# A trunk layer in split fp32: who splits the weights of the up product, the third branch and the projection, and who sums the stored blocks

## The chip, the cores and the metric

One core of a Trainium2 chip. The time is the device time of one execution in microseconds (us). The core's engines run side by side and meet through semaphores: TensorE (PE, matmuls into PSUM), VectorE (DVE), ScalarE (ACT), GpSimd (POOL), and SyncE (SP), whose queue issues most of the DMA transfers.

## The reference, cut to what matters

One decoder layer on x of 1024 tokens by 1024 features: three attention mixers, whose outputs pass a branch product each and are gated and summed, an output projection, and a squared-ReLU MLP. The change touches the end of the layer:

```python
y = jnp.einsum('nbsm,nmd->bsnd', branches, w_branch[layer])
gate = jax.nn.sigmoid(mg.reshape(B, S, N_BRANCH, D_MODEL).astype(jnp.float32)).astype(y.dtype)
x = x + jnp.sum(gate * y, axis=2) @ w_out[layer]

h = rms_norm(x, norm_mlp[layer])
x = x + jnp.square(jax.nn.relu(h @ w_up[layer])) @ w_down[layer]
```

All of it is fp32; w_branch[2] is the third branch, w_out the projection, w_up the up product (1024 by 4096).

## The kernel before, in words

**Splits.** Every fp32 operand of a matmul is split into a high and a low part: ScalarE casts the high part (L90), then VectorE or GpSimd subtracts it from the source (L91). `split` takes the engine as its last argument, `weight` loads a block and splits it, GpSimd being its default. A product then takes three matmuls, L119, L120 and L121. In the traces the high part of a weight is wh, the low part wl, a loaded raw block wr, a sum of blocks s.

**Third branch and projection.** The third branch (loop over two halves of the tokens and eight blocks d of features, L1230 and after) takes a weight, a gate g and a product, multiplies them (L1233), adds to y (L1235), and splits y into mh and ml (L1236, L1237). The projection's weights wo (eight blocks of two halves each, split at L1291) are loaded and split in the same stretch, and the projection itself follows.

**The up product.** w_up is cut into H = 16 pairs p. Each pair is one 2x2-block product done by a Strassen-like scheme with seven products, numbered 1 to 7; some take a raw block of w_up, others a sum of blocks (`sums`, L1267). A product is four steps of k with three matmuls each, 12 matmuls on 128x512 tiles. Products 2, 7 and 3 go on in the PSUM bank of products 1, 6 and 5, so before TensorE starts product 7 of a pair VectorE must have read product 6 out of the bank (L1416, u2 = product 6 + e1), and before product 3 it must have read product 5 (L1423, behind L1421, which reads product 7). Product 4 is added at L1426, product 3 at L1429, ScalarE applies ReLU and square (L1435, L1436). `store` then sums the finished blocks of the pair (again L1267, u from u) and sends the seven blocks to the DRAM tiles ud on SP's queue; SP's queue also loads the blocks of w_up.

**Order.** For the first HEAD = 4 pairs the products 1, 2 and 4 are done first, from raw blocks; then TensorE runs 6, 5, 7 of pair 0, 6 of pair 1, 3 of pair 0, 5 and 7 of pair 1, 6 of pair 2, 3 of pair 1, and so on; from pair 4 the products run pair by pair. TensorE's order is written by hand. Every other engine's order is set by a scheduler that plans the program on a timeline. `tc.issue_after(ins)` is a hold: what is written inside it stands behind `ins` in the order of the engine that runs `ins` (VectorE here); it doesn't wait for the end of `ins`. Before the change the products 6, 5, 7, 3 of the four pairs are held behind `last["sum"]` (L1332), the last sum of the activations' blocks.

**Buffers.** The raw blocks wr have 7 buffers, the sums s 5, the split weights 11 (3 + 8), the temporaries u 12, the copies of product 4 v 4. Each engine takes its instructions strictly in its own order.

Of the kernel before, what the change touches and what calls it, by code (L numbers as in the profile page):

```python
# [14 lines left out]
ALU = mybir.AluOpType  # L15
# [60 lines left out]
class Kernel:  # L76
# [1113 lines left out]
    def merge_and_mlp(self):  # L1190
        tc, nc, a = self.tc, self.nc, self.a
        kw = dict(bufs=1, reuse_waits="tile")
        halves = [slice(0, 512), slice(512, 1024)]
        mp = tc.alloc_tile_pool(name="mp", side="left", **kw)
        mh = mp.tile([P, KT, S], F32R, name="mh")
        ml = mp.tile([P, KT, S], F32R, name="ml")
        pre = tc.alloc_tile_pool(name="pre", side="right", **kw)
        self.wp = pre
        self.w_n, self.wr_bufs, self.w_bufs = 512, 3, 3
        with (tc.tile_pool(name="bb", side="right", **kw) as bb, tc.tile_pool(name="br", side="right", **kw) as br,  # L1200
              tc.tile_pool(name="bl", side="left", **kw) as bl, tc.tile_pool(name="bg", side="left", **kw) as bg,
              tc.tile_pool(name="wx", side="left", **kw) as wx):
            self.other = wx
            ob = [[bb.tile([P, S], F32R, name=f"ob{i}{x}") for x in range(2)] for i in range(4)]
            oc = [None, None]
            y = [None, None]
            for half, pool in ((0, br), (1, bl)):
                y[half] = pool.tile([P, KT, 512], F32, name="y")
                oc[half] = [[pool.tile([P, 512], F32R, name=f"oc{i}{x}") for x in range(2)] for i in range(4)]
            for s in halves:  # L1210
                for i in range(4):
                    self.operand(self.od[4 + i], s, *[x[:, s] for x in ob[i]])
            for d in range(KT):
                w = self.weight(a["wbr"][1, d], 512)
                if d == 1:
                    self.wo_after = self.last_load
                for half, s in enumerate(halves):
                    g = self.gate(bg, "g", 3, 1, d, s)
                    with tc.issue_after(self.last_gate):
                        nc.sync.dma_start(y[half][:, d], self.yd[d, :, s])  # L1220
                    ps = self.branch(1, d, [x[0][:, s] for x in ob], [x[1][:, s] for x in ob], w)
                    nc.vector.scalar_tensor_tensor(g, g, 1.0, ps, op0=ALU.add, op1=ALU.mult)
                    v = y[half][:, d, :]
                    nc.gpsimd.tensor_tensor(v, v, g, op=ALU.add)
            for half, s in enumerate(halves):
                for i in range(4):
                    self.operand(self.od[8 + i], s, *oc[half][i])
            for half, s in enumerate(halves):
                for d in range(KT):
                    w = self.weight(a["wbr"][2, d], 512)  # L1230
                    g = self.gate(bg, "g", 3, 2, d, s)
                    ps = self.branch(2, d, [x[0] for x in oc[half]], [x[1] for x in oc[half]], w)
                    nc.vector.scalar_tensor_tensor(g, g, 1.0, ps, op0=ALU.add, op1=ALU.mult)  # L1233
                    v = y[half][:, d, :]
                    nc.vector.tensor_tensor(v, v, g, op=ALU.add)  # L1235
                    nc.scalar.activation(mh[:, d, s], v, AF.Copy, scale=0.5)  # L1236
                    nc.vector.scalar_tensor_tensor(ml[:, d, s], v, 0.5, mh[:, d, s].bitcast(F32),  # L1237
                                                   op0=ALU.mult, op1=ALU.subtract)

        self.tail(mp, mh, ml, halves, pre)  # L1240
# [33 lines left out]
    def tail(self, mp, mh, ml, halves, pre):  # L1274
        tc, nc, a = self.tc, self.nc, self.a
# [9 lines left out]
        wo = [[wps[k // 4].tile([P, D], F32R, name=f"wo{k}{x}") for x in range(2)] for k in range(KT)]  # L1285
        for k in range(KT):
            r = xp.tile([P, D], F32, name="x1", tag="x1", bufs=2)
            with tc.issue_after(self.wo_after):
                nc.sync.dma_start(r, a["wo"][k])
            for s in halves:  # L1290
                self.split(wo[k][0][:, s], wo[k][1][:, s], r[:, s], nc.vector if k % 2 else nc.gpsimd)  # L1291
        nc.sync.dma_start(g, a["norm_mlp"].broadcast_to([P, D]))


# [43 lines left out]
        last = {}  # L1338
        HEAD = 4
# [24 lines left out]
        def form():  # L1364
            count["f"] += 1
            pool, bufs = (pre, 3) if main is None or count["f"] % 11 < 3 else (main, 8)
            return [pool.tile([P, 512], F32R, name=f"w{x}", tag=f"w{x}", bufs=bufs) for x in "hl"]
# [11 lines left out]
        def temp(tag="u"):  # L1379
            pool, bufs = dict(u=(more, 12), v=(more, 4), s=(main, 5), e=(main, HEAD))[tag]  # L1380
            return pool.tile([P, 512], F32, name=tag, tag=tag, bufs=bufs)

        def splitted(src, eng):
            f = form()
            self.split(*f, src, eng)
            return f
# [4 lines left out]
        def up_pair(p):  # L1391
            o = Pair()
            wu = lambda n: raw(a["wu"][p + H * (n[0] == "2"), :, (int(n[1]) - 1) * 512:int(n[1]) * 512])
            get = self.sums(wu, lambda: temp("s"), "s", nc.vector)
            o.ps, o.p4 = {}, None
            o.n = 0

            def product(i, chain=None, again=False):

                name = self.ASIDE[i]  # L1400
                w = splitted(wu(name) if again else get(name), nc.gpsimd)
                bh, bl, k0, s = moving[self.BSIDE[i]]
                ps = o.ps[i] = o.ps[chain] if chain else self.mm()
                for k in range(4):
                    ks = slice(k * P, k * P + P)
                    self.mm3(ps, w[0][:, ks], w[1][:, ks], bh[:, k0 + k, s], bl[:, k0 + k, s],
                             k == 0 and not chain, k == 3, bool(chain))

            def after(i):

                if i == 1:
                    o.e1 = temp("e")
                    nc.scalar.activation(o.e1, o.ps[1], AF.Copy)
                elif i == 6:
                    o.u2 = temp()
                    nc.vector.tensor_tensor(o.u2, o.ps[6], o.e1, op=ALU.add)  # L1416
                elif i == 2:
                    o.c11 = act(o.ps[2])
                elif i == 7:
                    u3 = o.u3 = temp()  # L1420
                    nc.vector.tensor_tensor(u3, o.ps[7], o.e1, op=ALU.add)  # L1421
                    c = temp()
                    nc.vector.tensor_tensor(c, o.ps[5], u3, op=ALU.add)  # L1423
                    o.c22 = act(c)
                elif i == 4:
                    nc.vector.tensor_tensor(o.u3, o.p4 or o.ps[4], o.u3, op=ALU.add)  # L1426
                    o.c21 = act(o.u3)
                elif i == 3:
                    nc.vector.tensor_tensor(o.u2, o.ps[3], o.u2, op=ALU.add)  # L1429
                    o.c12 = act(o.u2)  # L1430
                    store()

            def act(c):
                u = temp()
                nc.scalar.activation(u, c, AF.Relu)  # L1435
                nc.scalar.activation(u, u, AF.Square)  # L1436
                return u

            def store():

                blocks = {"11": o.c11, "12": o.c21, "21": o.c12, "22": o.c22}
                get = self.sums(lambda n: blocks[n], temp, "s", nc.vector)
                for i in self.ORDER:
                    nc.sync.dma_start(ud[p][i], get(self.ASIDE[i]))

            o.product, o.after = product, after
            return o

# [6 lines left out]
        pairs = [up_pair(p) for p in range(HEAD)]  # L1455
# [17 lines left out]
        for o in pairs:  # L1473
            o.product(4, None, True)
            o.p4 = temp("v")
            nc.scalar.activation(o.p4, o.ps[4], AF.Copy)
        with tc.issue_after(last["sum"]):
            for i, o in enumerate(pairs):
                up(o, (6,))
                if i:  # L1480
                    up(pairs[i - 1], (3,))
                up(o, (5, 7))
                o.after(4)
# [28 lines left out]
        for b in range(0, H, G):  # L1512
# [7 lines left out]
            for i in LAST if final else order:  # L1520
# [5 lines left out]
                if b and rest and count["x"] % 2 == 0:  # L1526
                    t, s = rest.pop(0)
                    r = main.tile([P, 512], F32, name="xr", tag="e", bufs=HEAD)
# [6 lines left out]
                for j in range(4):  # L1535
# [19 lines left out]
                    t, s = place[i](j)  # L1555
# [70 lines left out]
```

## Time and profile before

| | us |
|---|---|
| median of 3 runs | 1986.71 |
| the three runs | 1987.52, 1983.32, 1986.71 |
| the profiled execution | 1990.27 |
| its span in the trace | 1988.5 |
| PE busy | 1879.6 |
| DVE busy | 1420.5 |
| ACT busy | 1013.7 |
| POOL busy | 976.5 |

Times in the trace count from the start of the span. The third branch runs in about 1210 to 1255, the projection to about 1360, the up product's first four pairs from there to about 1440.

### The profile page before, as it was taken

The numbers are of one execution on the slowest core, as the hardware profiler recorded it, in microseconds if no ns is written. First come the engines' busy times: TensorE is split into PE (matmuls) and PEld (weight loads), VectorE is DVE, ScalarE is ACT, GpSimd is POOL, SyncE is SP. The second block draws the span as 40 slices with busy tenths as digits, with TensorE's granted clock in tenths as the row PEclk, the third lists the DMA queues.
The fourth block names the chain that finished last, engine by engine and source line by source line (L and its number), as shares of the span: only waits on it lengthen the run. The fifth ranks groups of instructions, "written<-read, shape, count | busy, mean of one in ns | idle before, by whom it ended". The sixth has DMA issues, their size and how long they took to land. (4 is left out here: it accounts for less than half of the span.)

```text
span 1988.5 us, 30626 instructions
## 1 busy us (share of the span) xinstructions
PE 1879.6 (95%) x9842; PEld 1611.2 (81%) x9842; DVE 1420.5 (71%) x3196; ACT 1013.7 (51%) x2566; POOL 976.5 (49%) x1146
## 2 busy tenths in 40 slices
PE   7999999998899999999999889999899999999998
PEld 6888889887688888888888778887688888887886
DVE  7747777788657677658776756657755446899988
ACT  5456555666546555536556533335455546543432
POOL 4455455643361122172222237328454555889787
PEclk9999999999999999999999899999999999999999
DMA  6132012101201111202342557425544446455443
GB/s 225 52 107 57 9 57 55 53 16 55 84 27 63 52 52 58 79 19 93 100 127 94 172 168 256 158 86 166 170 170 158 147 155 207 159 179 181 129 154 111
DMA packets 124924, 221.58 MB, mean 111 GB/s; under 512 B 14708, under 2 KB 35732, under 8 KB 124764
## 3 DMA queue, kind: packets, MB, share of 16 engines
q1 hardware_dynamic: 123180, 213.87, 33.0%
q10 hardware_dynamic: 1584, 5.77, 0.9%
q8 instruction: 77, 1.26, 0.3%
q14 instruction: 83, 0.68, 0.1%
HBM read 158.68 MB, written 64.83 MB: 112 GB/s over the span
## 5 line engine op out<-in xcount | busy, mean ns | idle before, releaser
L91 POOL TENSOR_TENSOR wl<-wr,wh 128x512 fp32r<-128x512 f32 (+3 forms) x246 | 329.3, 1345 | 264.6 <-ACT wh L90 212.7
L90 ACT ACTIVATE wh<-wr 128x512 fp32r<-128x512 f32 (+3 forms) x258 | 149.9, 589 | 183.4 <-PE mm L120 111.9
L716 PE MATMUL sc<-st 128*128 128x256 f32 (+6 forms) x736 | 182.5, 341 | 20.8 <-ACT p L748 20.1
L90 ACT ACTIVATE ph<-tr 128x384 fp32r<-128x384 f32 (+3 forms) x280 | 138.6, 497 | 118.6 <-PE tr L764 97.5
L91 DVE TENSOR_TENSOR pl<-tr,ph 128x384 fp32r<-128x384 f32 (+3 forms) x280 | 155.7, 559 | 33.1 <-ACT ph L90 31.1
L119 PE MATMUL mm<-hh,wh 128*128 128x512 f32 x384 | 159.0, 414 | 0.0
L761 POOL MEMSET ph<- 128x128 f32 x152 | 33.7, 222 | 252.3 <-PE ac L904 220.1
L716 PEld LDWEIGHTS sc<-st 128*128 128x128 f32 x736 | 122.1, 191 | 41.0 <-ACT p L748 32.0
L120 PE MATMUL mm<-hl,wh 128*128 128x512 f32 x384 | 151.6, 395 | 0.0
L121 PE MATMUL mm<-hh,wl 128*128 128x512 f32 x384 | 151.5, 395 | 0.0
L119 PE MATMUL mm<-wh 128*128 128x512 f32 x352 | 138.2, 393 | 3.4 <-DVE x L1499 3.4
L120 PE MATMUL mm<-wl,wh 128*128 128x512 f32 x352 | 138.3, 393 | 2.1 <-POOL wl L91 2.0
L90 ACT ACTIVATE wh<-u 128x512 fp32r<-128x512 f32 x158 | 90.7, 621 | 93.2 <-PE tr L120 35.0
L121 PE MATMUL mm<-wh,wl 128*128 128x512 f32 x352 | 137.9, 392 | 0.0
L764 PE MATMUL tr<-ident,p 128*128 128x128 f32 x792 | 128.8, 275 | 8.7 <-DVE st L569 7.4
L91 POOL TENSOR_TENSOR wl<-s,wh 128x512 fp32r<-128x512 f32 x68 | 94.8, 1401 | 77.6 <-ACT wh L90 76.6
L748 ACT ACTIVATE p<-sc,mc 128x256 f32<-128x256 f32 (+5 forms) x200 | 106.7, 539 | 47.2 <-DVE mc L740 43.1
L904 PE MATMUL ac<-ph,st 128*128 128x256 f32 x392 | 109.8, 298 | 19.6 <-DVE ob L911 13.4
L91 DVE TENSOR_TENSOR wl<-u,wh 128x512 fp32r<-128x512 f32 x98 | 115.7, 1181 | 11.1 <-ACT wh L90 10.9
L119 PE MATMUL mm<-wh,hh 128*128 128x384 f32 (+1 forms) x320 | 115.7, 361 | 0.6 <-ACT raw L525 0.6
L905 PE MATMUL ac<-pl,st 128*128 128x256 f32 x392 | 106.4, 292 | 7.2 <-DVE pl L91 7.0
L120 PE MATMUL mm<-wl,hh 128*128 128x384 f32 (+1 forms) x320 | 109.1, 341 | 0.0
(320 smaller groups left out, 5742.4 us busy)
## 6 DMA issues: line engine op xcount, KB each, us to landing
ud<-u SPq DMA_DIRECT2D x112, 256.0 KB, 2.3
u<-ud SPq DMA_DIRECT2D x98, 256.0 KB, 3.7
wr<-wu SPq DMA_DIRECT2D x76, 256.0 KB, 2.8
wr<-wd SPq DMA_DIRECT2D x64, 256.0 KB, 2.9
gd<-go SPq DMA_DIRECT2D x48, 256.0 KB, 2.0
g<-gd SPq DMA_DIRECT2D x48, 256.0 KB, 3.3
wr<-wg SPq DMA_DIRECT2D x40, 256.0 KB, 2.7
wr<-wbr SPq DMA_DIRECT2D x40, 256.0 KB, 3.3
```

What stands on the lines that cost most here:

```text
L90: nc.scalar.activation(hi, src, AF.Copy)
L91: (eng or nc.vector).tensor_tensor(lo, src, hi.bitcast(F32), op=ALU.subtract)
L119: mm(out, lh, rh, start=first, stop=False, skip_group_check=more)
L120: mm(out, lh, rl, start=False, stop=False, skip_group_check=more)
L121: mm(out, ll, rh, start=False, stop=last, skip_group_check=more)
L716: self.nc.tensor.matmul(ps[:, off:off + k1 - k0], q[:, t * P:(t + 1) * P], k[:, k0:k1], start=i == 0, stop=i == 1)
L748: self.last_exp = self.nc.scalar.activation(p, ps, AF.Exp, bias=m, scale=-1.0, accum_out=l).ins
L761: nc.gpsimd.memset(ph[0:rows, o:o + P].bitcast(F32), 0.0)
L764: nc.tensor.transpose(pt[0:rows, o:o + P], src, self.ident)
L904: nc.tensor.matmul(ac, v, ph, start=first, stop=False)
L905: nc.tensor.matmul(ac, v, pl, start=False, stop=last)
```

## The change

Five edits. The third branch's 16 weight splits go from GpSimd to VectorE; the projection's splits, which alternated between the two, all go to GpSimd. The splits of the sums for products 6, 5, 7 and 3 of the first four pairs (16) go from GpSimd to VectorE, the raw ones (1, 2 and 4) stay. The sums of the stored blocks of these pairs (4 each, 16) go from VectorE to GpSimd. And pairs 2 and 3 are held behind pair 0's L1416, pairs 0 and 1 behind `last["sum"]` as before.

```diff
-                    w = self.weight(a["wbr"][2, d], 512)
+                    w = self.weight(a["wbr"][2, d], 512, nc.vector)
...
-                self.split(wo[k][0][:, s], wo[k][1][:, s], r[:, s], nc.vector if k % 2 else nc.gpsimd)
+                self.split(wo[k][0][:, s], wo[k][1][:, s], r[:, s], nc.gpsimd)
...
-                w = splitted(wu(name) if again else get(name), nc.gpsimd)
+                w = splitted(wu(name) if again else get(name), nc.vector if p < HEAD and not again else nc.gpsimd)
...
-                    nc.vector.tensor_tensor(o.u2, o.ps[6], o.e1, op=ALU.add)
+                    o.evicted = nc.vector.tensor_tensor(o.u2, o.ps[6], o.e1, op=ALU.add).ins
...
-                get = self.sums(lambda n: blocks[n], temp, "s", nc.vector)
+                get = self.sums(lambda n: blocks[n], temp, "s", nc.gpsimd if p < HEAD else nc.vector)
...
-        with tc.issue_after(last["sum"]):
-            for i, o in enumerate(pairs):
+        for i, o in enumerate(pairs):
+            with tc.issue_after(pairs[0].evicted if i > 1 else last["sum"]):
                 up(o, (6,))
```

TensorE's order is the same before and after. On VectorE, at the start of the third branch (L1222 is the second branch's gate, L1233 to L1237 the third's), before:

```order
L1222 SCALAR_TENSOR_TENSOR g<-g,mm 128x512 x7
L91 TENSOR_TENSOR wo_15416<-x_15435,wo_15415 128x512 x2
L1233 SCALAR_TENSOR_TENSOR g<-g,mm 128x512
L1235 TENSOR_TENSOR y<-y,g 128x512
L1233 SCALAR_TENSOR_TENSOR g<-g,mm 128x512
L1237 SCALAR_TENSOR_TENSOR ml<-y,mh 128x512
```

and after, from the same place:

```order
L1222 SCALAR_TENSOR_TENSOR g<-g,mm 128x512
L91 TENSOR_TENSOR wl<-wr,wh 128x512
L1222 SCALAR_TENSOR_TENSOR g<-g,mm 128x512
L91 TENSOR_TENSOR wl<-wr,wh 128x512
L1222 SCALAR_TENSOR_TENSOR g<-g,mm 128x512
L91 TENSOR_TENSOR wl<-wr,wh 128x512
L1222 SCALAR_TENSOR_TENSOR g<-g,mm 128x512 x2
L91 TENSOR_TENSOR wl<-wr,wh 128x512
L1222 SCALAR_TENSOR_TENSOR g<-g,mm 128x512 x2
L91 TENSOR_TENSOR wl<-wr,wh 128x512
L1233 SCALAR_TENSOR_TENSOR g<-g,mm 128x512
L91 TENSOR_TENSOR wl<-wr,wh 128x512
```

The projection's splits (wo) left VectorE, and the third branch's weight splits (wl from wr) stand in their stead, the first six of them among the second branch's gates.

On VectorE, around the up product's first eviction L1416, before (s is a sum of w_up's blocks):

```order
L1267 TENSOR_TENSOR s<-s,wr 128x512
L1267 TENSOR_TENSOR s<-wr 128x512 x2
L1267 TENSOR_TENSOR s<-s,wr 128x512
L1267 TENSOR_TENSOR s<-wr,s 128x512
L1267 TENSOR_TENSOR s<-wr 128x512 x2
L1267 TENSOR_TENSOR s<-s,wr 128x512
L1267 TENSOR_TENSOR s<-wr,s 128x512
L1267 TENSOR_TENSOR s<-wr 128x512 x2
L1267 TENSOR_TENSOR s<-s,wr 128x512
L1267 TENSOR_TENSOR s<-wr,s 128x512
L1267 TENSOR_TENSOR s<-wr 128x512
L1267 TENSOR_TENSOR s<-wr,s 128x512
L1416 TENSOR_TENSOR u<-mm,e 128x512
```

and after (a first s<-wr stands just ahead of this, as before):

```order
L1267 TENSOR_TENSOR s<-s,wr 128x512
L1267 TENSOR_TENSOR s<-wr 128x512
L91 TENSOR_TENSOR wl<-s,wh 128x512 x3
L1267 TENSOR_TENSOR s<-wr 128x512
L1267 TENSOR_TENSOR s<-s,wr 128x512
L1267 TENSOR_TENSOR s<-wr,s 128x512
L1267 TENSOR_TENSOR s<-wr 128x512
L91 TENSOR_TENSOR wl<-s,wh 128x512 x4
L1416 TENSOR_TENSOR u<-mm,e 128x512
```

The sums of pairs 2 and 3 moved behind L1416, and seven splits (three of pair 0, four of pair 1) came ahead of it. Behind it, the next VectorE instructions up to pair 0's L1423 are, after:

```order
L1267 TENSOR_TENSOR s<-wr 128x512
L1267 TENSOR_TENSOR s<-s,wr 128x512
L1267 TENSOR_TENSOR s<-wr,s 128x512
L1267 TENSOR_TENSOR s<-wr 128x512
L91 TENSOR_TENSOR wl<-s,wh 128x512
L1267 TENSOR_TENSOR s<-wr 128x512
L91 TENSOR_TENSOR wl<-s,wh 128x512 x3
L1267 TENSOR_TENSOR s<-s,wr 128x512
L1421 TENSOR_TENSOR u<-mm,e 128x512
L1267 TENSOR_TENSOR s<-wr,s 128x512
L1267 TENSOR_TENSOR s<-wr 128x512
L1423 TENSOR_TENSOR u<-mm,u 128x512
```

Before, only two sums and L1421 stood between L1416 and L1423 of pair 0.

On GpSimd, in the up product, before:

```order
L91 TENSOR_TENSOR wl<-wr,wh 128x512
L91 TENSOR_TENSOR wl<-s,wh 128x512 x15
L91 TENSOR_TENSOR wl<-wr,wh 128x512
L91 TENSOR_TENSOR wl<-s,wh 128x512 x3
L91 TENSOR_TENSOR wl<-wr,wh 128x512
```

and after, from the same place (u are the blocks to be stored):

```order
L91 TENSOR_TENSOR wl<-wr,wh 128x512 x2
L1267 TENSOR_TENSOR u<-u 128x512 x3
L91 TENSOR_TENSOR wl<-s,wh 128x512
L1267 TENSOR_TENSOR u<-u 128x512
L91 TENSOR_TENSOR wl<-s,wh 128x512
L91 TENSOR_TENSOR wl<-wr,wh 128x512
L1267 TENSOR_TENSOR u<-u 128x512
```

The splits of the four pairs' sums left GpSimd, and the store sums stand between its splits for the later pairs.

## Rows read from the trace of the kernel before

**Rows 1.** The page's head and its first part: busy time, share of the span and instructions of each engine.

```profile
span 1988.5 us, 30626 instructions
PE 1879.6 (95%) x9842; PEld 1611.2 (81%) x9842; DVE 1420.5 (71%) x3196; ACT 1013.7 (51%) x2566; POOL 976.5 (49%) x1146
```

**Rows 2.** TensorE's waits in 1345 to 1440: the line waited for, us in total, how often, the longest.

```profile
PE mm L119 <- DVE u L1416: 8.9, 1, 8.9
PE mm L119 <- DVE u L1423: 1.5, 1, 1.5
```

**Rows 3.** Busy time of each engine in stretches of 10 us (instructions in brackets), then the granted TensorE clock, the DMA engines' share and GB/s.

```profile
1380.00:1390.00 10.00, 8.67 (x39) 6.84 (x37) 8.56 (x6) 6.50 (x13) 10.00 (x7) 1.00 0.65 217
1390.00:1400.00 10.00, 2.48 (x6) 1.99 (x7) 8.63 (x8) 1.26 (x2) 6.32 (x4) 0.56 0.56 176
1400.00:1410.00 10.00, 10.00 (x43) 8.16 (x42) 5.66 (x7) 5.36 (x9) 3.88 (x3) 0.93 0.31 106
```

**Rows 4.** The same columns (PE, PEld, DVE, ACT, POOL, clock, DMA share, GB/s) for single microseconds.

```profile
1388.00:1389.00 1.00, 0.67 (x3) 0.20 (x2) 1.00 (x2) 0.86 (x2) 1.00 (x1) 1.00 0.71 229
...
1390.00:1391.00 1.00, 0.00 (x0) 0.00 (x0) 0.91 (x2) 0.00 (x0) 1.00 (x1) 1.00 0.90 299
1391.00:1392.00 1.00, 0.00 (x0) 0.00 (x0) 0.99 (x2) 0.05 (x1) 1.00 (x2) 0.60 0.71 207
...
1402.00:1403.00 1.00, 1.00 (x6) 0.82 (x5) 0.60 (x1) 0.63 (x1) 0.07 (x1) 1.00 0.00 0
1427.00:1428.00 1.00, 0.05 (x1) 0.00 (x0) 0.97 (x3) 0.00 (x0) 0.00 (x0) 1.00 0.30 109
```

**Rows 5.** The chain of waits in 1380 to 1432: start, duration, what.

```profile
1397.53 0.79 PE mm L119
...
1400.88 0.43 PE mm L120
...
1401.66 0.23 PE mm L119
...
1425.37 1.70 DVE s L1267
...
1427.70 0.70 DVE u L1423
1428.54 0.47 PE mm L119
```

**Rows 6.** VectorE's timeline in the up product: start, duration, instruction, count; in square brackets the idle time before it and what ended it.

```profile
1368.90 1.79 DVE L1267 TENSOR_TENSOR s<-s,wr 128x512 f32<-128x512 f32 x1
1370.62 3.50 DVE L1267 TENSOR_TENSOR s<-wr 128x512 f32<-128x512 f32 x2
...
1377.82 0.94 DVE L1267 TENSOR_TENSOR s<-wr,s 128x512 f32<-128x512 f32 x1 [2.00 <-DMA wr<-wu]
...
1386.84 3.35 DVE L1267 TENSOR_TENSOR s<-wr 128x512 f32<-128x512 f32 x2
...
1395.12 1.74 DVE L1267 TENSOR_TENSOR s<-wr,s 128x512 f32<-128x512 f32 x1
1396.79 0.68 DVE L1416 TENSOR_TENSOR u<-mm,e 128x512 f32<-128x512 f32 x1
1397.39 0.68 DVE L1267 TENSOR_TENSOR s<-wr 128x512 f32<-128x512 f32 x1
1398.16 0.69 DVE L1267 TENSOR_TENSOR s<-s,wr 128x512 f32<-128x512 f32 x1
...
1421.77 3.60 DVE L1267 TENSOR_TENSOR u<-u 128x512 f32<-128x512 f32 x4 [1.36 <-ACT u L1436]
```

**Rows 7.** GpSimd's timeline there, the same columns.

```profile
1373.53 1.73 POOL L91 TENSOR_TENSOR wl<-wr,wh 128x512 fp32r<-128x512 f32 x1
1375.22 21.10 POOL L91 TENSOR_TENSOR wl<-s,wh 128x512 fp32r<-128x512 f32 x13
1402.93 1.29 POOL L91 TENSOR_TENSOR wl<-s,wh 128x512 fp32r<-128x512 f32 x1 [6.61 <-ACT wh L90]
```

**Rows 8.** TensorE's waits in 1245 to 1300, columns as in rows 2.

```profile
PE mm L121 <- POOL wl L91: 0.9, 1, 0.9
```

**Rows 9.** VectorE's groups by line in 1210 to 1270: count, busy us, mean ns of one, then the idle time before.

```profile
L1235 DVE TENSOR_TENSOR y<-y,g 128x512 f32<-128x512 f32 x16 | 16.5, 1032 | 0.2
L1237 DVE SCALAR_TENSOR_TENSOR ml<-y,mh 128x512 fp32r<-128x512 f32 x16 | 15.4, 961 | 2.7 <-ACT mh L1236 2.1
L91 DVE TENSOR_TENSOR wo<-x,wo 128x512 fp32r<-128x512 f32 x8 | 11.8, 1502 | 1.2 <-ACT wo L90 1.2
L1233 DVE SCALAR_TENSOR_TENSOR g<-g,mm 128x512 f32<-128x512 f32 x16 | 10.8, 676 | 1.0 <-DMA g<-gd 1.0
```

**Rows 10.** GpSimd's groups by line in 1210 to 1270, the same columns.

```profile
L91 POOL TENSOR_TENSOR wl<-wr,wh 128x512 fp32r<-128x512 f32 x14 | 22.5, 1615 | 9.7 <-PE mm L121 5.8 <-ACT wh L90 2.3 <-issue 1.2
L91 POOL TENSOR_TENSOR wo<-x,wo 128x512 fp32r<-128x512 f32 x8 | 13.9, 1754 | 2.4 <-ACT wo L90 2.4
```

**Rows 11.** VectorE's store sums in 1355 to 1445, from the groups by line and form.

```profile
L1267 DVE TENSOR_TENSOR u<-u 128x512 f32<-128x512 f32 x12 | 10.9, 950 | 2.8 <-ACT u L1436 2.7
```

**Rows 12.** The page's sixth part, the stores of the up product: queue, count, KB each, median us from issue to landing.

```profile
ud<-u SPq DMA_DIRECT2D x112, 256.0 KB, 2.3
```

**Rows 13.** GpSimd's groups by line in 1400 to 1445, columns as in rows 9.

```profile
L91 POOL TENSOR_TENSOR wl<-s,wh 128x512 fp32r<-128x512 f32 x10 | 14.0, 1402 | 21.4 <-ACT wh L90 21.4
L91 POOL TENSOR_TENSOR wl<-wr,wh 128x512 fp32r<-128x512 f32 x5 | 7.0, 1395 | 5.8 <-ACT wh L90 5.8
```

## The prediction

> **What bounds the kernel now.** I read the page's span and busy rows first [rows 1]: TensorE is busy 1879.6 of 1988.5 us, VectorE 71%. So TensorE's waits set the time, and an engine's share of busy time decides nothing unless TensorE waits for it. Next I read TensorE's waits around the stage that the change rewrites [rows 2]: one wait of 8.9 us for L1416 (the eviction of pair 0's product 6) and one of 1.5 us for L1423. The table of stretches [rows 3] shows the first as TensorE 2.48 busy of 10 in 1390-1400. Microsecond by microsecond [rows 4], work stops within 1388-1389 (0.67 busy, so at 1388.67); the granted clock is still 1.00 in 1390-1391, 0.60 in 1391-1392 and back at 1.00 only in 1402-1403. The chain of waits [rows 5] shows the price of that half clock: matmuls stand 0.43 us apart up to 1401.66 and 0.23 after it.
>
> Why is L1416 late? Product 6 of pair 0 ended one product before 1388.67. A product is 12 matmuls of 0.23, 2.75 us, so that was about 1385.9. VectorE, however, was still making sums for pairs that TensorE wants much later, and each took about 1.7 us while GpSimd worked: 3.35 for two, 1.74 for one, then L1416 at 1396.79. As soon as GpSimd's 13 splits end (1375.22 + 21.10 = 1396.3), the same sum takes 0.68 to 0.69 [rows 6, 7].
>
> **The change part by part.** *The stall.* The order puts L1416 behind the sums of pairs 0 and 1 and seven splits, and the sums of pairs 2 and 3 behind it. VectorE has made the third of these sums by about 1372.4 (the first of the two in 1370.62 + 3.50). Seven splits and four sums remain. GpSimd's last raw split ends at 1375.2, so two of the eleven run at 1.75 (3.5 us) and nine at 0.69 (6.2): 1382.1. A raw block that landed at 1377.82 delays one sum but fits into this. The last of these splits needs the buffer of the product that ends at 1388.67 - 2 x 2.75 = 1383.2, so it ends at 1383.9. L1416 then waits only for product 6 itself and ends at about 1386.6, before TensorE asks at 1388.67. The 8.9 us go. With them goes the half clock: nine matmuls took 1401.66 - 1397.53 = 4.13 us against 9 x 0.23 = 2.07, so 2.1 us. If all eleven operations ran at 1.75, L1416 would end at 1372.4 + 19.3 + 0.7 = 1392.4 (the second rival).
>
> *The wait at 1427.* The sums of stored blocks (3.60 for four from 1421.77, and 1.70 for a sum behind them) stand ahead of L1423 on VectorE [rows 5, 6]. They leave VectorE: 1.5 us, and the 0.2 by which the first matmul after a wait is longer (0.47 against 0.23), go.
>
> *Third branch and projection.* VectorE gains 16 splits and loses 8; GpSimd the reverse. TensorE's one wait near there is 0.9 us for a GpSimd split [rows 8]. In 1210-1270 VectorE is busy with 16.5 + 15.4 + 11.8 + 10.8 = 54.5 us in these four groups [rows 9], so it is nearly full, and the exchange adds operations there. By the order six of its 16 new splits stand among L1222 and the first L1233, ahead of this stretch, and GpSimd has no third-branch splits (1615 ns each) but the 16 of the projection, 16 x 1.754 = 28.1 us [rows 10]. While it works, 28.1 / 1.75 = 16 of VectorE's operations meet it at 1.75; the other 10 + 32 - 16 = 26 run at 0.69, L1233 as now: 28.0 + 17.9 + 10.8 = 56.7 us, 2.2 more than now, into 60 - 54.5 = 5.5 us without such work. So the last L1237 comes no later, and I cost the exchange at nothing: -0.9 and no new wait. If that cover is gone, TensorE waits by the excess: bounds 0 and 2.2.
>
> *What the change adds: waits of pair 0's L1423.* Eight sums and four splits for pairs 2 and 3 are queued behind L1416 and ahead of L1423 of pair 0, with L1421: 13 operations, which follow each other by 0.60 where GpSimd rests (1396.79 to 1397.39 [rows 6]) and take 0.69 one by one: 7.8 to 9.0 us from 1386.6, plus 0.7 for L1423 itself, 1395.1 to 1396.3. TensorE wants pair 0's product 3 after product 7 and pair 1's product 6: 1388.67 + 5.5 = 1394.2. Wait 0.9 to 2.1, and 2.4 if one operation meets GpSimd's two remaining splits; I take 1.5, the middle.
>
> *L1423 of pair 1* now waits for a buffer: GpSimd makes the store sums one by one (1.29 alone [rows 7], against 0.95 on VectorE [rows 11]), and the store must land (2.3 us [rows 12]) before the buffer is free. Two sums and a landing after pair 0's last activation: 2 x 1.29 + 2.3 = 4.9 us, against four products of cover minus the activation's chain. Bounds 0 to 2.3; I take 1.0.
>
> *L1423 of pairs 2 and 3* stand behind sums that wait for a free block from GpSimd's splits. GpSimd there has 15 splits at 1.40 and 27.2 us idle in 45 [rows 13]; 16 store sums are added. At 1.40 they are 31 x 1.40 = 43.4 of 45 us: they just fit. At the pace beside a busy VectorE, 21.10 / 13 = 1.62 [rows 7], they are 50.2: 5.2 too many. VectorE loses those 16 sums, so it meets GpSimd less often, which is nearer to 1.40. Bounds 0 to 5.2; I take 1.2.
>
> [...]
>
> *The sum*, on the profiled execution: 8.9 + 2.1 + 1.5 + 0.2 + 0.9 = 13.6 removed, 1.5 + 1.0 + 1.2 = 3.7 added, 9.9 gained: 1990.27 - 9.9 = 1980.4. That execution is 3.56 above the median of the three runs (1986.71), so on the median's scale **1976.8 us**. The added waits have the ends 0.9 and 2.4 + 2.3 + 5.2 = 9.9; the three upper ends rarely come together, and two thirds of it, 6.5, is as far as I let the forecast go. Its own range is then 1974.0 to 1979.6, and the spread of the three runs (4.2 us) widens its lower end to 1972.
>
> **The rivals.** *First, the waits move on:* L1423 of each of the four pairs stays late, at 2 us a pair, because GpSimd's sums and the stores' landing replace VectorE's. Added 8 instead of 3.7: gain 5.6, **1981.1**. For it: four pairs have the same pattern and the buffers are few. Against it: pairs 2 and 3 have no held sums ahead of them.
>
> *Second, the splits don't fit ahead of product 7* (the change then does not do what its order says): all eleven at 1.75, L1416 at 1392.4, 3.7 us of stall left and the half clock with it (2.1). Gain 13.6 - 3.7 - 5.8 = 4.1, **1982.6**. Against it: the 0.68 of VectorE's sums once GpSimd rests [rows 6].
>
> *Third, many small waits throttle the clock.* Four waits of about 1 us would each bring the 2.1 us at half clock: 8.4 more, gain 1.5, **1985.2**. Against it speaks the wait at 1427: TensorE 0.05 busy in 1427-1428, clock 1.00 [rows 4]. [...]
>
> *Fourth, on the other side: GpSimd becomes the bound.* The place is 1400-1445. 31 operations in 45 us are 7.6, say 8, for the 11.0 us of one pair's four products. At 1.75, the time of a projection split beside VectorE [rows 10], a pair takes 14.0: 3.0 us late, in four pairs 12. Such a stall is longer than the 2.5 us after which the clock fell here (1388.67 to 1391.2, where a mean of 0.60 over 1391-1392 puts the step from 1.00 to 0.50 [rows 4]), so each brings 2.1 more: 20.4 in place of 3.7. 1990.27 - 13.6 + 20.4 = 1997.1, **1993.5** on the median's scale. It begins to cost from 11.0 / 8 = 1.38 per operation and turns the change into a loss from about 1.68 (2.4 us late and the clock). Against it: 1.40 in that stretch now, with fewer VectorE sums after.
>
> The clock's part of it hangs on the 2.5 us. [...]
>
> **How the numbers follow.** Forecast 0.66, first rival 0.13, second 0.08, third 0.03, fourth 0.10. A measurement of this kernel can tell about 0.2%, 4 us, from no change. Faster by more: all of the forecast, 0.09 of the first and 0.03 of the second: 0.78. Within: 0.04, 0.05, the third 0.03 and 0.01 of the fourth: 0.13. Slower: 0.09. The range goes from 1972 to 1984, over the first two rivals, and leaves out most of the third and the fourth, about 0.15 with the unlikely lower end.
>
> **What would show it.** Right: TensorE's wait for L1416 gone and the clock at 1.00 through 1385-1402; a wait of about 1 us for L1423 in its place; GpSimd with almost no idle time in the 45 us that follow, at about 1.4 per operation; no wait for a GpSimd split near 1255. Wrong: a clock below 1.00 there, waits of over 2 us for L1423 or a sum, GpSimd's mean at 1.6 or more, VectorE late with the last L1237 of the third branch. What would make the forecast wrong altogether is a VectorE that still needs 1.7 us for an operation ahead of L1416.

## The result and the profile after

| | us |
|---|---|
| before, median of 6 runs | 1986.74 (1983.32 to 1990.91) |
| changed, median of 6 runs | 1974.16 (1969.44 to 1977.13) |
| ratio, 95% interval | 0.9933 (0.9921 to 0.9944) |
| profiled execution, changed | 1972.63, span 1970.7 |

The change is faster by 12.6 us, 0.67%; 1976.8 was forecast, with 1972 to 1984 as the range. Two later timings of the same kernel, beside other kernels below, gave 11.2 and 11.3 us.

TensorE's waits in 1345 to 1440, where [rows 2] had 8.9 and 1.5:

```profile
PE mm L119 <- DVE u L1423: 3.3, 4, 1.3
```

The wait for L1416 is gone; four short waits for L1423 have come, none above 1.3 us. In 1245 to 1300, where [rows 8] had 0.9, the view lists no wait at all. The stretches that answer to [rows 3] (PE, PEld, DVE, ACT, POOL, clock, DMA share, GB/s):

```profile
1380.00:1390.00 10.00, 8.77 (x40) 6.92 (x39) 10.00 (x17) 5.71 (x10) 0.38 (x1) 1.00 0.72 217
1390.00:1400.00 10.00, 8.68 (x39) 6.90 (x38) 7.36 (x12) 4.43 (x9) 7.80 (x6) 1.00 0.57 210
1400.00:1410.00 10.00, 9.67 (x43) 7.67 (x41) 6.95 (x7) 4.38 (x7) 10.00 (x8) 1.00 0.64 211
```

The clock is 1.00 throughout. GpSimd, 10.00 busy in 1380-1390 of before, has 0.38 there now, and 10.00 in 1400-1410, where it had 3.88. The same events come about 9.3 us earlier in this trace than in that of before. VectorE's timeline, which answers to [rows 6]:

```profile
1362.99 4.09 DVE L91 TENSOR_TENSOR wl<-s,wh 128x512 fp32r<-128x512 f32 x3
1367.00 0.68 DVE L1267 TENSOR_TENSOR s<-wr 128x512 f32<-128x512 f32 x1
...
1372.08 1.38 DVE L91 TENSOR_TENSOR wl<-s,wh 128x512 fp32r<-128x512 f32 x2 [0.18 <-issue]
1376.71 0.69 DVE L1416 TENSOR_TENSOR u<-mm,e 128x512 f32<-128x512 f32 x1 [3.26 <-PE mm L121]
...
1381.06 1.89 DVE L91 TENSOR_TENSOR wl<-s,wh 128x512 fp32r<-128x512 f32 x3
...
1385.27 0.68 DVE L1423 TENSOR_TENSOR u<-mm,u 128x512 f32<-128x512 f32 x1
...
1395.56 0.69 DVE L1421 TENSOR_TENSOR u<-mm,e 128x512 f32<-128x512 f32 x1 [1.19 <-POOL u L1267]
1397.67 0.69 DVE L1423 TENSOR_TENSOR u<-mm,u 128x512 f32<-128x512 f32 x1 [1.42 <-DMA ud<-u]
...
1407.02 1.76 DVE L1267 TENSOR_TENSOR s<-wr,s 128x512 f32<-128x512 f32 x1 [2.43 <-POOL wl L91]
```

L1416 waits 3.26 us for product 6 to end, and TensorE no longer waits for L1416: the splits ahead of it were done at 1373.5. From 1377 to 1394 sums and splits follow each other by 0.60 us, where before a sum took 1.7. GpSimd's timeline, for [rows 7], shows why:

```profile
1364.19 1.73 POOL L91 TENSOR_TENSOR wl<-wr,wh 128x512 fp32r<-128x512 f32 x1
1389.62 1.70 POOL L91 TENSOR_TENSOR wl<-wr,wh 128x512 fp32r<-128x512 f32 x1 [23.70 <-DVE wl L91]
1393.45 4.68 POOL L1267 TENSOR_TENSOR u<-u 128x512 f32<-128x512 f32 x3 [2.12 <-ACT u L1436]
```

It rests for 23.7 us, does one split, and begins the store sums at 1393.45, when VectorE is all but through with the work of pairs 2 and 3. Its groups in 1400 to 1445, for [rows 13]:

```profile
L1267 POOL TENSOR_TENSOR u<-u 128x512 f32<-128x512 f32 x13 | 19.8, 1530 | 0.0
L91 POOL TENSOR_TENSOR wl<-s,wh 128x512 fp32r<-128x512 f32 x10 | 13.6, 1356 | 2.3 <-ACT wh L90 2.3
L91 POOL TENSOR_TENSOR wl<-wr,wh 128x512 fp32r<-128x512 f32 x7 | 10.4, 1490 | 1.1 <-ACT wh L90 1.1
```

30 operations in 43.8 us are 1.46 each, with 3.4 us idle where there were 27.2.

**Where the profiled span lost 17.8 us.** From 1988.5 to 1970.7 the two profiled executions differ by more than the medians. ScalarE's first L1236, in the third branch, is a landmark behind a program that is the same up to about 1200. Before, and then after (start, duration, instruction):

```profile
1218.52 0.63 ACT L1236 ACTIVATE mh<-y 128x512 fp32r<-128x512 f32 x1 [4.07 <-DVE y L1235]
```

```profile
1210.56 0.63 ACT L1236 ACTIVATE mh<-y 128x512 fp32r<-128x512 f32 x1 [3.99 <-DVE y L1235]
```

8.0 us were gained ahead of the landmark; 1988.5 - 1218.52 = 770.0 from there to the end became 760.1, a gain of 9.8. Over the 14 profiled executions of this study the landmark lies between 1208.85 and 1218.52, and two repeats of the changed kernel have it at 1218.27 and 1214.06: the 8.0 us are scatter and not the change. Part of this scatter goes with the clock. Added up from the clock column in stretches of 5 us, TensorE had half clock ahead of the landmark for 34.1 us in before and 13.6 in the changed kernel; over 0 to 1200 the mean clock is 0.98 in the repeat whose landmark is at 1218.27 and 0.99 in the other 13. By each profiled execution's span and mean clock, less the half clock in 1370 to 1430, this time and the landmark correlate by 0.77 over the 14. So I read each experiment by two numbers: its ratio, and the time from the landmark to its end (the rest, below), which leaves this scatter out. The changed kernel's three profiled executions have a rest of 760.1, 760.5 and 760.1.

Two more landmarks show where the 9.8 us lie: VectorE's first sum of the up product and the L1423 of its fourth pair (pair 3). Before, and then after:

```profile
1366.59 0.69 DVE L1267 TENSOR_TENSOR s<-wr 128x512 f32<-128x512 f32 x1 [2.27 <-DMA wr<-wu]
...
1438.60 0.69 DVE L1423 TENSOR_TENSOR u<-mm,u 128x512 f32<-128x512 f32 x1
```

```profile
1357.26 0.69 DVE L1267 TENSOR_TENSOR s<-wr 128x512 f32<-128x512 f32 x1 [2.27 <-DMA wr<-wu]
...
1420.77 0.69 DVE L1423 TENSOR_TENSOR u<-mm,u 128x512 f32<-128x512 f32 x1
```

From L1236 to the first sum 148.1 us became 146.7 (1.4 gained, third branch and projection), from there to pair 3's L1423 72.0 became 63.5 (8.5, the up product), and from there to the end it is 549.9 in both.

### The profile page after: what moved, and what is told of

Read it like the earlier page. It is cut to its first block, busy times and chain, and to the rows that moved or that the text cites. A ratio compares the mean times of both kernels' runs of the same rounds, so it can differ in the third digit from the quotient of the medians.

```text
span 1970.7 us, 30611 instructions
## 1 busy us (share of the span) xinstructions
PE 1870.3 (95%) x9842; PEld 1604.5 (81%) x9842; DVE 1415.6 (72%) x3204; ACT 1014.2 (51%) x2566; POOL 964.2 (49%) x1138
## 5 line engine op out<-in xcount | busy, mean ns | idle before, releaser
L91 POOL TENSOR_TENSOR wl<-wr,wh 128x512 fp32r<-128x512 f32 (+3 forms) x230 | 306.2, 1339 | 264.3 <-ACT wh L90 196.8
L121 PE MATMUL mm<-wh,hl 128*128 128x384 f32 (+1 forms) x320 | 108.9, 340 | 0.0
```

The source lines that it names most:

```text
L91: (eng or nc.vector).tensor_tensor(lo, src, hi.bitcast(F32), op=ALU.subtract)
L121: mm(out, ll, rh, start=False, stop=last, skip_group_check=more)
```

## The experiments

All were timed in five rounds beside the kernel before. Waits are TensorE's idle times in the up product.

| kernel | median, before beside it | ratio (95%) | waits for L1416; L1423 | rest |
|---|---|---|---|---|
| before | | | 8.9; 1.5 | 770.0 |
| x1_branch | 1984.48, 1986.39 | 0.9992 (0.9979 to 1.0005) | 8.4; 1.5, and 0.5 for L1435 | 769.6 |
| x2_up | 1978.47, 1986.39 | 0.9961 (0.9945 to 0.9977) | none; 3.4 | 763.4 |
| x3_hold | 1984.30, 1986.39 | 0.9990 (0.9974 to 1.0006) | none; 7.4 | 771.5 |
| x4_no_hold | 1979.12, 1986.39 | 0.9961 (0.9945 to 0.9976) | 4.6; 0.2 | 762.8 |
| y0_again | 1974.29, 1985.45 | 0.9947 (0.9928 to 0.9966) | none; 3.4 | 760.5 |
| y1_store_dve | 1977.68, 1985.45 | 0.9960 (0.9947 to 0.9973) | none; 4.5 | 762.1 |
| y2_hold_1423 | 1981.16, 1985.45 | 0.9975 (0.9963 to 0.9986) | none; 6.7 | 765.6 |
| y3_hold_store0 | 1979.62, 1985.45 | 0.9969 (0.9955 to 0.9983) | none; 0.4, and 7.3 for wh | 766.3 |
| z1_hold_pair3 | 1979.46, 1986.59 | 0.9968 (0.9950 to 0.9986) | none; 6.0 | 763.6 |
| z2_pair3_store0 | 1978.27, 1986.59 | 0.9966 (0.9950 to 0.9983) | none; 6.5 | 766.0 |
| z3_split_pool | 1979.96, 1986.59 | 0.9963 (0.9947 to 0.9978) | 1.1; 5.7 | 764.1 |
| z4_again | 1975.32, 1986.59 | 0.9942 (0.9920 to 0.9964) | none; 3.3 | 760.1 |

### One half of the change at a time

**x1_branch**, the two branch edits on the kernel before:

```diff
-                    w = self.weight(a["wbr"][2, d], 512)
+                    w = self.weight(a["wbr"][2, d], 512, nc.vector)
...
-                self.split(wo[k][0][:, s], wo[k][1][:, s], r[:, s], nc.vector if k % 2 else nc.gpsimd)
+                self.split(wo[k][0][:, s], wo[k][1][:, s], r[:, s], nc.gpsimd)
```

> Only the third branch's splits on VectorE and the projection's on GpSimd. My theory (the gain sits in the up product, in the order and pace of VectorE ahead of L1416): the 0.9 us wait near 1250 goes, the 8.9 us wait for L1416 stays with its half clock; 0.5 to 1.5 us faster than before, ratio 0.9993 to 0.9997. Rival (these two edits give the 3 us by which the measured gain exceeds the 9.4 us that the trace shows in the two changed stages): 3 to 4 us faster, ratio 0.998.

1.9 us faster, within its interval of no change. The third branch has no wait; L1416 is waited for as before. Both theories' sizes lie in the interval, so the time alone does not decide; the rest of 769.6 against 770.0 speaks for the small one. By the landmarks this kernel wins 1.3 us up to the first sum (146.8 against 148.1), but its first L1423 comes 184.4 us after L1236, as before (184.6). I take it that while the stall for L1416 stands, its end and not the third branch sets when the up product goes on.

**x2_up**, the other edits without these two (on the kernel before: `nc.vector if p < HEAD and not again` for the splits, `nc.gpsimd if p < HEAD` for the store sums, and the hold):

> Only the up product's edits (splits of the sums on VectorE, store sums on GpSimd, the hold). My theory: the 8.9 us wait goes, four waits of together about 3.3 us for L1423 stay, the 0.9 us wait near 1250 stays; 8 to 9 us faster than before, ratio 0.9955 to 0.996. Rival (the branch edits matter more): under 8 us faster. Should it be 11 to 12 us faster, then the extra 3 us over the trace's sum belong to the up product.

7.9 us faster, on the line of 8 between theory and rival. The waits in the up product are the changed kernel's (3.4 in four). The third branch keeps its waits, and more of them than in the trace of before, in 1200 to 1300:

```profile
PE mm L121 <- POOL wl L91: 2.8, 4, 0.9
```

x3_hold, which has the old third branch too, shows 1.6 us there. From L1236 to the first sum these two take 150.4 and 150.2 us, before took 148.1, and the kernels with both branch edits take 146.0 to 147.3. So the branch edits look worth 1.4 to 3.7 us where I priced 0.9; whether the trace of before was a low draw, one profile of it cannot show.

### The parts of the up product

**x3_hold**, the hold alone:

```diff
-                    nc.vector.tensor_tensor(o.u2, o.ps[6], o.e1, op=ALU.add)
+                    o.evicted = nc.vector.tensor_tensor(o.u2, o.ps[6], o.e1, op=ALU.add).ins
...
-        with tc.issue_after(last["sum"]):
-            for i, o in enumerate(pairs):
+        for i, o in enumerate(pairs):
+            with tc.issue_after(pairs[0].evicted if i > 1 else last["sum"]):
```

> Only the hold: pairs 2 and 3 stand behind pair 0's L1416, every split and sum stays on its old engine. Theory: L1416 comes in time (the sums of pairs 0 and 1 were done by 1380.5 in the trace of before), but seven sums of pairs 2 and 3, at 1.7 us beside GpSimd's splits, now stand ahead of pair 0's L1423: 1386.7 + 7 x 1.7 + 1.4 = 1400 against 1394.2, so a wait of 4 to 6 us there with the half clock; gain 2 to 6 us, ratio 0.997 to 0.999. Rival A (the hold is the whole change): a wait of 1 us and a gain of 8 to 9 us, ratio 0.9955. Rival B (the split's engine is the whole change): nothing, ratio 1.000.

The wait for L1416 is gone by the hold alone, and almost nothing is won: TensorE now waits 2.0 us for pair 0's L1423 and 4.1 for pair 1's, and each of the two is followed by half clock (3.4 us of it after the first, 6.8 with the second; the rows stand in the last section). VectorE's timeline:

```profile
1381.07 3.48 DVE L1267 TENSOR_TENSOR s<-wr 128x512 f32<-128x512 f32 x2
...
1389.54 1.76 DVE L1267 TENSOR_TENSOR s<-wr,s 128x512 f32<-128x512 f32 x1
1391.23 1.76 DVE L1426 TENSOR_TENSOR u<-v,u 128x512 f32<-128x512 f32 x1
1392.91 1.78 DVE L1267 TENSOR_TENSOR s<-wr 128x512 f32<-128x512 f32 x1
...
1398.73 4.68 DVE L1267 TENSOR_TENSOR u<-u 128x512 f32<-128x512 f32 x4 [0.16 <-ACT u L1436]
...
1404.65 0.69 DVE L1423 TENSOR_TENSOR u<-mm,u 128x512 f32<-128x512 f32 x1
```

The held sums only stand in the way in another place, at 1.7 us beside GpSimd's splits, and the store sums stand in the way of pair 1's L1423. I had the size of the wait right and its place half: pair 0's was 2.0, not 4 to 6.

**x4_no_hold**, all edits but the hold (`with tc.issue_after(last["sum"])` round the whole loop, as before):

> All of the change but the hold: VectorE makes the sums and splits of all four pairs ahead of pair 0's L1416. Theory: with GpSimd at rest each takes 0.6, but some 14 more operations stand ahead of L1416 than in the changed kernel, and their raw blocks land late: L1416 at 8 to 9 us after its place there, 5 to 7 us later than TensorE wants it; a stall of 4 to 7 us and half clock; gain 3 to 7 us, ratio 0.9965 to 0.9985. Rival B (the pace alone mends it): no wait for L1416 and the full gain, ratio 0.993 to 0.995.

A wait of 4.6 us for L1416 stays, 7.3 us are won. With GpSimd at rest (0.00 busy in 1370 to 1390) VectorE makes the work of all four pairs in 0.6 us steps, but some sums wait for their raw blocks:

```profile
1382.64 0.69 DVE L1267 TENSOR_TENSOR s<-wr,s 128x512 f32<-128x512 f32 x1 [1.45 <-DMA wr<-wu]
...
1385.31 0.68 DVE L1416 TENSOR_TENSOR u<-mm,e 128x512 f32<-128x512 f32 x1
```

So pace and order each end part of the stall, and neither alone all of it.

**z3_split_pool**, the changed kernel with the sums' splits on GpSimd again:

```diff
-                w = splitted(wu(name) if again else get(name), nc.vector if p < HEAD and not again else nc.gpsimd)
+                w = splitted(wu(name) if again else get(name), nc.gpsimd)
```

> The changed kernel, but the splits of the sums stay on GpSimd: hold, store sums on GpSimd, and the branch edits. Theory (the splits' engine is needed because GpSimd's splits slow VectorE's sums to 1.7 us and GpSimd must also make the store sums): waits for L1423 of pairs 0 and 1 of together 6 to 10 us, with half clock; gain 0 to 4 us, ratio 0.998 to 1.000. Rival (the hold and the store sums suffice): waits of 3 to 4 us, ratio 0.9945 to 0.9955.

Neither side was right: the waits for L1423 are 5.7 us (2.0 and 3.5 of it for pairs 0 and 1, where the theory expected 6 to 10 and the rival 3 to 4 in all) and 1.1 for L1416, and 6.6 us are won where the theory allowed 4. I had charged half clock for every wait, and here only the longest, 3.5 us, lost it.

**y1_store_dve**, the changed kernel with the store sums on VectorE:

```diff
-                get = self.sums(lambda n: blocks[n], temp, "s", nc.gpsimd if p < HEAD else nc.vector)
+                get = self.sums(lambda n: blocks[n], temp, "s", nc.vector)
```

> The changed kernel, but the sums of the stored blocks stay on VectorE. Theory (GpSimd's 31 operations in 45 us and its late store sums make the waits for L1423 of pairs 1 to 3, VectorE has room): GpSimd idles again, the waits for L1423 after the first fall from 2.1 to under 1 in total; 0 to 1.5 us faster than the changed kernel. Rival (VectorE is then the bound there: some 20 operations a pair by 0.62 are 12.4 against 11.0): waits of 1 to 2 us a pair, 3 to 6 us slower than the changed kernel.

My theory fell, the rival held: two waits, of 1.2 and 3.2 us, and 3.4 us slower than the changed kernel by the medians, where the rival had 3 to 6; by the rest it is 1.6 to 2.0. VectorE's timeline ahead of pair 1's L1423:

```profile
1399.01 1.90 DVE L1267 TENSOR_TENSOR u<-u 128x512 f32<-128x512 f32 x3
1400.81 0.69 DVE L1421 TENSOR_TENSOR u<-mm,e 128x512 f32<-128x512 f32 x1
1402.07 1.74 DVE L1267 TENSOR_TENSOR s<-s,wr 128x512 f32<-128x512 f32 x1 [0.57 <-POOL wl L91]
1403.73 0.68 DVE L1423 TENSOR_TENSOR u<-mm,u 128x512 f32<-128x512 f32 x1
```

The store sums and one sum that waits 0.57 us for GpSimd's split and then takes 1.74 stand ahead of the eviction.

### The changed kernel again, and tries to beat it

**y0_again** and **z4_again** are the changed kernel as it stands, without an edit.

> The changed kernel itself, timed again beside the next three. In the profiled runs of the last four kernels the program up to 1200, which is the same in all of them, took 4 to 8 us less than in the profiled run of before, and the waits of the third branch in the two kernels that leave it alone were 2.8 and 1.4 us in place of 0.9. Theory: the change is worth what its two stages show, 8.5 in the up product and 1 to 3 in the third branch, and the 12.6 was at the lucky end: 9.5 to 11.5 us, ratio 0.9942 to 0.9952. Rival (something that no stage shows brings 3 us more): 12 to 13.5 us again, ratio 0.9932 to 0.994.

> The changed kernel once more, beside these three. Theory: 10 to 12 us faster than before, ratio 0.994 to 0.9955, and four waits for L1423 of together 3.3 to 3.4 us in the trace. Rival (12.6 is its true gain): ratio 0.9932 to 0.994.

11.2 and 11.3 us, both within what the theories allowed (9.5 to 11.5, and 10 to 12) and below the rivals' 12 and 12.6; the same four waits each time.

The first of the four waits, 1.2 us for pair 0's L1423, looks easy to remove. Three kernels hold the later pairs otherwise; `freed` is the `.ins` of L1423:

```diff
-            with tc.issue_after(pairs[0].evicted if i > 1 else last["sum"]):
+            with tc.issue_after(pairs[0].freed if i > 1 else last["sum"]):
```

**y2_hold_1423** is this edit, **y3_hold_store0** has pair 0's store sums on VectorE besides (`nc.gpsimd if 0 < p < HEAD`).

> The changed kernel, but pairs 2 and 3 are held behind pair 0's L1423 and not its L1416. Theory: the wait of 1.2 us for pair 0's L1423 goes, since no sum stands ahead of it any more; the sums and splits of pair 2, some eight operations by 0.6 from 1383, are done by 1390, before TensorE wants them at 1394; 1.2 to 1.5 us faster than the changed kernel. Rival (the held work is late instead): a wait for a split or L1416 of pairs 1 or 2 of 1 to 4 us, the same or up to 3 us slower.

> The hold behind pair 0's L1423, and the store sums of pair 0 alone back on VectorE. Theory: both the 1.2 us wait of pair 0 and the 1.3 us wait of pair 1 (L1421 and L1423 waited there for a GpSimd store sum and its landing) go: 2 to 3 us faster than the changed kernel. Rival: pair 0's four store sums on VectorE delay pair 1's L1423 by as much: 1 us faster at most.

Both theories fell, and the cost is larger than either rival had it: pair 0's wait is gone, but the held work is late, and pair 1's product 3 waits 6.4 us for L1423, in the other kernel 7.3 for the cast of a weight whose sum VectorE made late (L1423 ended only 0.15 us before TensorE went on). Both are slower than the changed kernel by 5 to 7 us by the medians.

**z1_hold_pair3** holds only pair 3 at L1423 (`pairs[0].freed if i > 2 else pairs[0].evicted if i > 1 else last["sum"]`), **z2_pair3_store0** the same with pair 0's store sums on VectorE.

> The changed kernel, but only pair 3 is held later, behind pair 0's L1423; pair 2 stays behind pair 0's L1416. Theory (in the kernel that held both pairs behind L1423, VectorE idled 4.7 us ahead of L1421 and the work then came too late for pair 1's L1423; here it makes pair 2's eight operations in that gap): the 1.2 us wait for pair 0's L1423 goes, pair 1's stays at about 1.3; total waits 2.1 in place of 3.4 in the trace, about 1 us faster than the changed kernel, ratio to before 0.9935 to 0.995. Rival: any held work comes late again, a wait of 3 to 7 us for pair 1's L1423, ratio 0.9965 to 0.998.

> The same with pair 0's store sums on VectorE. Theory: pair 1's L1423 no longer waits for GpSimd's store sum and its landing, but for four more operations by 0.6 on VectorE, 2.4 us, against the 2.6 that it waited for GpSimd and the store: even, waits of 1 to 2 us in total, ratio 0.993 to 0.995. Rival: VectorE is the bound at that place, a wait of 3 us or more for pair 1's L1423, ratio 0.9955 or more.

Again the rivals: 5.8 and 6.5 us for pair 1's L1423. VectorE in z1_hold_pair3:

```profile
1384.34 0.69 DVE L1423 TENSOR_TENSOR u<-mm,u 128x512 f32<-128x512 f32 x1
...
1390.36 2.93 DVE L91 TENSOR_TENSOR wl<-s,wh 128x512 fp32r<-128x512 f32 x3
1393.21 1.78 DVE L1267 TENSOR_TENSOR s<-wr 128x512 f32<-128x512 f32 x1
1394.91 1.78 DVE L91 TENSOR_TENSOR wl<-s,wh 128x512 fp32r<-128x512 f32 x1
1396.61 1.75 DVE L1267 TENSOR_TENSOR s<-s,wr 128x512 f32<-128x512 f32 x1
...
1401.93 0.69 DVE L1423 TENSOR_TENSOR u<-mm,u 128x512 f32<-128x512 f32 x1
```

and GpSimd:

```profile
1392.61 5.20 POOL L1267 TENSOR_TENSOR u<-u 128x512 f32<-128x512 f32 x3 [1.08 <-ACT u L1436]
```

Pair 0's L1423 is in time, so pair 0's blocks are finished earlier, and GpSimd begins their sums 2.9 us earlier than in the changed kernel, counted from L1236 (180.0 against 182.9 us), while VectorE has pair 3's work later, behind L1423. From 1392.6 a sum or split that meets GpSimd costs VectorE 1.75 in place of 0.60. So I read the changed kernel's 1.2 us wait as the price for GpSimd starting only when VectorE is nearly done. None of these versions beats the changed kernel.

## Why the prediction was right

**The stall and the half clock (11.0 of the 13.6).** Right. VectorE is ready for L1416 3.26 us before product 6 ends, and the clock stays at 1.00. My path to it holds: eleven operations, two of the first splits beside GpSimd (4.09 for three, as allowed), the rest at 0.6 to 0.7. I had the last split end at 1383.9 on before's time scale; 1373.5 is 1382.8 there, the events being 9.3 earlier. The second rival (all at 1.75) did not come about, because GpSimd rests for 23.7 us. x3_hold and x4_no_hold show that it takes both the order and that rest.

**The added waits, 3.7 forecast, 3.3 measured.** Pair 0's L1423: 1.5 forecast, 1.2 measured. Pair 1's: 1.0 and 1.3, and for the reason given, since L1421 waits 1.19 for GpSimd's store sum and L1423 1.42 for a store to land. Pairs 2 and 3: 1.2 together, and 0.8 remain of the 3.3, behind sums that wait up to 2.43 for GpSimd's splits; the 1.5 at 1427, behind store sums, is gone. For the last two terms I had chosen a value inside bounds of 0 to 2.3 and 0 to 5.2, so that they came so near is in part luck. y2_hold_1423 and z1_hold_pair3 remove pair 0's wait by taking held work from ahead of it, and y1_store_dve, which relieves GpSimd, has no wait for pairs 2 and 3: these sit on the queues named here. For pair 1 the rows above are the evidence, since every kernel that touched its wait put a longer one in its place. The first rival's 8 us of such waits did not come, nor the third's lost clock: four waits of up to 1.3 us left it at 1.00.

**The branch edits.** The 0.9 went, with nothing new. The size was low: up to the first sum the changed kernel is 1.4 us shorter than before, and the old third branch waits 0.9, 1.6 and 2.8 us in three traces, so these edits may be worth 0.5 to 2.8 us more than I priced. VectorE is not late there; it is busy 51.35 of 60 us in 1210-1270.

**The fourth rival** put GpSimd's limit at 1.38 us per operation. It ran at 1.46 in that stretch and no lag of over 0.6 us reached TensorE. The limit was drawn too low by rounding 7.6 operations to 8: 11.0 / 7.6 = 1.45. So the change works at the edge of this engine.

**The size.** 9.9 forecast; 9.8 by the rest of the trace, 12.6 by the medians. That the first two agree to 0.1 is luck: the up product gave 8.5 where the terms make 9.0, the third branch and projection 1.4 where they make 0.9. The difference of 2.8 sits, in the profiled executions, ahead of the landmark, where the program is the same and the scatter is 9.7 us. The repeats, 11.2 and 11.3, have intervals (0.9928 to 0.9966, 0.9920 to 0.9964) that take in 9.8 us, 0.9951; the first one (0.9921 to 0.9944) does not. If other executions of before spend as long up to the first sum as x2_up and x3_hold do, 2 us more than the one in its profile, the gain is about 12. That is an argument and not shown; where the 1.4 to 2.8 us between the rest and the three timings come from stays open.

## What to carry to other kernels

A hold that lets urgent work pass is worth what the queue behind it can bear: count the operations that it puts ahead of the next urgent one, at the pace that they will have then. Moving work between two engines that slow each other is paid by when they overlap, not by their totals; here the same sums cost 0.6 or 1.75 us. A short wait that keeps the two apart can be cheaper than its removal: before it is removed, look at what its end will start.

## What the hardware showed that I had not expected

The clock's loss was not in proportion to the wait. Stretches that show it, for waits of 3.2 us (y1_store_dve), 4.6 (x4_no_hold) and 5.8 (z1_hold_pair3), in this order:

```profile
1400.00:1410.00 10.00, 6.77 (x23) 5.10 (x23) 6.34 (x9) 3.77 (x7) 3.54 (x3) 0.83 0.55 192
```

```profile
1380.00:1390.00 10.00, 5.37 (x18) 4.04 (x17) 7.05 (x11) 1.94 (x4) 0.00 (x0) 0.83 0.59 184
```

```profile
1400.00:1410.00 10.00, 7.24 (x21) 5.78 (x22) 6.51 (x8) 4.12 (x7) 4.88 (x4) 0.66 0.72 236
```

At half clock (0.50 in the single microseconds 1402 to 1404 of z1_hold_pair3 and 1404 to 1406 of x3_hold), a mean of 0.83 over 10 us is 2 x 0.17 x 10 = 3.4 us, 0.66 is 6.8; before, 0.56 and 0.93 in [rows 3] make 10.2. It came in pieces of 3.4 us: in 1370 to 1430 the 14 profiled executions have 0, 3.4, 6.8 or 10.2 of it. The length of the wait alone did not decide how many. Two kernels have a wait of 2.0 us for pair 0's L1423 in 1380 to 1390. In x3_hold it is followed by one piece, from about 1389.8 (0.99 in the first row below is 0.2 us of it), 1.3 us after L1423 had ended at 1388.53, and the 4.1 us wait behind it brings two more:

```profile
1380.00:1390.00 10.00, 8.00 (x36) 6.26 (x35) 9.91 (x10) 4.87 (x9) 9.49 (x6) 0.99 0.49 155
1390.00:1400.00 10.00, 10.00 (x39) 8.15 (x38) 9.80 (x10) 4.98 (x9) 6.14 (x5) 0.84 0.59 186
1400.00:1410.00 10.00, 5.91 (x18) 4.40 (x17) 7.80 (x10) 2.83 (x5) 3.54 (x3) 0.67 0.57 204
```

In z3_split_pool the same wait is followed by none, in spite of one of 1.1 us behind it:

```profile
1380.00:1390.00 10.00, 8.01 (x36) 6.17 (x34) 9.91 (x9) 4.44 (x8) 10.00 (x6) 1.00 0.57 181
1390.00:1400.00 10.00, 6.00 (x26) 4.43 (x24) 7.14 (x9) 3.74 (x7) 6.66 (x6) 1.00 0.57 182
```

In the up product of these kernels waits of up to 1.5 us never lost the clock, those of 3.2 us and more always did. So the 2.5 us of my fourth rival is no threshold, and my price of 2.1 us for each wait above it fits long ones only: waits of 3.2, 3.5 and 4.6 us lost one piece, at most 1.7 us of work. Nor did a longer wait always lose more: 6.4 us (y2_hold_1423) lost three pieces and 7.3 (y3_hold_store0) two. Waits of 2.0 (x3_hold) and 3.2 us (y1_store_dve), each shorter than a piece, were enough for one.

The slowing of VectorE beside GpSimd shows in splits and sums alike: 1.75 to 1.78 in z1_hold_pair3 from 1393.21, against 0.68 for a sum at 1384.95 there, while GpSimd rested. Operations that read PSUM did not slow: L1421 took 0.69 at 1395.56 in the changed kernel, inside GpSimd's three store sums (1393.45 to 1398.13), and 0.68 at 1401.16 in z1_hold_pair3, inside another (1.71 from 1400.65). The 1.62 that the prediction took as GpSimd's pace beside a busy VectorE was read wrongly: VectorE did rest beside those 13 splits (8.56 and 8.63 busy of 10 in [rows 3]), so 1.62 mixes splits that met it with splits that did not. In z1_hold_pair3, where they met, each side took about 1.75: three store sums took 5.20 us beside VectorE's operations of 1.75 to 1.78. That is no fixed share: in y2_hold_1423 GpSimd's four store sums from 1391.61 took 9.82 us, 2.46 each, while three VectorE sums inside them, from 1391.92, took 0.69 each.
